# A two-layer hybrid decoder on one core: bonus and bias folded into the value projection, shorter roots, A blocks ahead of the output, r's loads first

## The chip, the cores and the metric

One core of a Trainium2 chip runs the whole kernel. The metric is the device time of one execution in microseconds (us), the median of several runs; a separate execution is recorded by the profiler. The engines are TensorE (PE, with its weight loads as PEld), VectorE (DVE), ScalarE (ACT), GpSimd (POOL) and SyncE (SP), whose queue starts most of the DMA transfers; ACT and POOL have DMA queues of their own.

## The reference

1024 tokens of width 1024 pass two layers, everything in float32. Layer 0 is RWKV-7 time mixing and a squared-ReLU MLP, layer 1 is causal attention with forget gates on shared keys and values and a second MLP. What the change touches:

```python
rkv = jnp.einsum('pbtd,pde->pbte', jnp.stack([x_r, x_k, x_v]), w_rkv)
...
y = (y - mean) * lax.rsqrt(var + GN_EPS)
y = y.reshape(B, T, D) * lnx_w.astype(f32) + lnx_b.astype(f32)
bonus = jnp.sum(r_h * k_h * r_k.astype(f32), axis=-1, keepdims=True) * v_h
y = (y + bonus.reshape(B, T, D)).astype(h.dtype) * g
return y @ w_o
```

Here `y` is the output of the recurrence over tokens (16 heads with a 64x64 state each), normalized per head; the bonus is one number per token and head times v. Keys and queries of the attention layer are normalized per head too, `rmsnorm(k, k_norm_g)`.

## The kernel before

Every float32 product is done as three matmuls of numbers split in two parts: a rounded part (`hi`, `whi`; made by ACT, L744) and the rest (`lo`, `wlo`; a subtraction, L747, on an engine that the caller names). The stages follow one another, and each engine works through its own queue in order. A scheduler makes these queues from the program's order and priorities, and for parts of the kernel (`k.pe`, the recurrence among them) PE keeps the order in which the program is written.

- **Start (0 to 84 us).** x's eight row blocks are loaded, each is normalized (`rsqrt_small`, L86 to L92: v = x*scale + eps, ACT's Ln and Exp, and four DVE steps that refine the root), transposed by PE (L889), and projected.
- **k and r (84 to 325).** Projections in blocks of 128 columns (`proj_pairs`, matmuls at L838). For each block of k, POOL, DVE and ACT make decays (`E`), scaled keys (`KK`, `kr`, `BK`) and the small matrices `N`, which go to DRAM (`d_E`, `d_KR`, `d_BK`, `d_N`). For each block of r, `prep_receptance` loads `Er` and `kr` (L286, L289; tiles of which three exist), `receptance` multiplies r with Er (L299) and forms the bonus (L300; sums over a head by PE at L203, copied by ACT at L211, four copies a block). DVE also inverts triangular blocks there (L316, L318: `Nb`, `Tb`, `Tm`, loaded at L309). SP's queue holds the loads and stores of all of this. In r and v the subtraction `wlo` is made by POOL; in k by DVE.
- **v (325 to 421).** `proj_tokens` (L858) computes 256 columns (g) for 256 tokens (b) at a time; `emit_v` copies them out (L975) and stores them in `d_v`. Beside it, DVE and ACT make the mixed input of the gates (`xg`; `t` at L923 and L924, `hi`, `lo`).
- **Recurrence (459 to about 745).** 16 chunks of 64 tokens. PE's order in a chunk c is: `pp`, `yp` from `KRz` (`rec_solve`; the state's part of the output), a transpose `tp`, `sa`, blocks `ap` of the next chunk (`rec_blocks`; DVE masks them into `AE`, L429), `u` (`rec_state`; DVE adds St into Z, L503; POOL scales St, L508), `yp` from `AE` (`rec_out`, the rest of the output), the second half of the blocks `ap`, and then `op` (`rec_corner`), which needs `AE`. Then DVE and POOL normalize the output (`rec_norm`: sum `m` L531, scaling L532, subtraction L533, root L86 to L92, product L540; on POOL the weight L541, the bias lnb L542, v times bonus L543, the sum L544), and POOL scales `KRz` for the next chunk (L455), as DVE scales AE (L455). From the fourth chunk on PE has 24 matmuls of the output projection (`wo`) per chunk to fill with, before that some of the gates (`gp`). `psA`, `psC` and `psY` are PSUM pools.
- **Keys, queries, values (1440 to 1644).** Products in Strassen form. `leave` copies a finished half (ACT), `emit` normalizes it per head (`hss`, `hrs`, L1708 to L1712: two feature halves, each with a root of its own) and has it transposed (L370) after four more products. Weights are scaled by the norm's gain in `w`, on engines that the string "wg" lists, otherwise DVE (L77).
- **Attention (1660 to 1895).** Head pairs: `b` and `d` hold the gate's bias (`dg` made by POOL, L1946), scores `s`, maximum `mx` (DVE, L1836), softmax on ACT, transposes `pt`.

The table that names engines for this stage has one letter per operation: v, s and p for DVE, ACT and POOL. The functions touched:

Of the kernel before, what the change touches and what calls it, by code (L numbers as in the profile page):

```python
# [56 lines left out]
        "wl": "vpvpvpvvvvpvpv", "wf": "pvvvvpvv", "wg": "vvvpvvsvvvvvssss"},  # L57
# [22 lines left out]
def rsqrt_small(k, pool, out, x, scale, eps, tag=""):  # L80

    nc = k.nc
    shape = list(x.shape)
    v = pool.tile(shape, F32, tag="rs_v" + tag, name="rs_v")
    t = pool.tile(shape, F32, tag="rs_t" + tag, name="rs_t")
    nc.vector.tensor_scalar(v, x, scale, eps, op0=ALU.mult, op1=ALU.add)  # L86
    nc.scalar.activation(t, v, AF.Ln)
    nc.scalar.activation(out, t, AF.Exp, scale=-0.5)
    nc.vector.tensor_tensor(t, v, out, op=ALU.mult)
    nc.vector.tensor_tensor(t, t, out, op=ALU.mult)  # L90
    nc.vector.tensor_scalar(t, t, -0.5, 1.5, op0=ALU.mult, op1=ALU.add)
    nc.vector.tensor_tensor(out, out, t, op=ALU.mult)  # L92


def make_consts(k):
    nc = k.nc
    cp = k.const
    k.ident = cp.tile([P, P], F32, name="ident")
    make_identity(nc, k.ident)

# [53 lines left out]
def rwkv_keep(k):  # L154

    cp, dr = k.const, k.dram

    k.sc = cp.tile([P, NK, NCH], F32, name="sc")
    k.ns2 = cp.tile([P, NK, NCH], F32, name="ns2")
    k.bon = cp.tile([P, NK, NCH], F32, name="bon")  # L160
    k.d_KR = dr.tile([NCH, P, NK, 2, C], F32, name="d_KR")
    k.d_BK = dr.tile([NCH, P, NK, 2, C], F32, name="d_BK")

    k.d_N = [dr.tile([2, P, 32, 32], F32, name=f"d_N{i}") for i in range(2)]
    k.d_E = [dr.tile([P, HC, C + 1], F32, name=f"d_E{i}") for i in range(2 * NK)]
    k.d_T = dr.tile([NK * 64, 32, 32], F32, name="d_T")
    k.d_B = dr.tile([NK * 64, 32, 32], F32, name="d_B")
# [90 lines left out]
def prep_pair(k, p, units):  # L258
# [10 lines left out]
    for h in range(2):  # L269
# [3 lines left out]
        for c in range(2):  # L273
            for d in range(2):
                s0 = u % 4 * 32 + (c * 2 + d) * HC
                q = 64 * c + 32 * d
                nc.sync.dma_start(k.d_N[p // 4][u // 4, s0:s0 + HC].rearrange("c i t -> i c t"),
# [4 lines left out]
def prep_receptance(k, p, hf, pool):  # L282

    cc = slice(HC * hf, HC * hf + HC)
    E = pool.tile([P, HC, C + 1], F32, tag="o", name="Er", bufs=3)
    k.nc.sync.dma_start(E, k.d_E[2 * p + hf])  # L286
    kt = pool.tile([P, HC, C], F32, tag="v", name="kr", bufs=3)
# [38 lines left out]
def rec_pools(k, ctx, a):  # L326
# [26 lines left out]
    k.lnb = k.rc.tile([P, NK, C], F32, name="lnb")  # L353
    for t, ap in ((k.lnw, a["rwkv_lnx_w"][0]), (k.lnb, a["rwkv_lnx_b"][0])):
# [165 lines left out]
def rec_norm(k, s):  # L520
# [5 lines left out]
    for h in range(2):  # L526
        nc.sync.dma_start(V[64 * h:64 * h + 64], k.d_v[cs, :].rearrange("t (p h v) -> h t p v", h=2, v=C)[h])
# [4 lines left out]
    nc.vector.tensor_scalar_mul(m, m, 1.0 / C)  # L532
    nc.vector.tensor_tensor(Y, yp, m.unsqueeze(2).broadcast_to(S3), op=ALU.subtract)  # L533
# [8 lines left out]
    nc.gpsimd.tensor_tensor(Y, Y, k.lnb, op=ALU.add)  # L542
    nc.gpsimd.tensor_tensor(V, V, k.bon[:, :, c:c + 1].broadcast_to(S3), op=ALU.mult)  # L543
# [21 lines left out]
def stage_recurrence(k, a, tile_of, gates):  # L565
    nc, tc = k.nc, k.tc
    with ExitStack() as ctx:
# [107 lines left out]
        for c in range(NCH):  # L675
# [18 lines left out]
            rec_out(k, cur, Z)  # L694
            if more:
                prepare(nxt, "b")
                hook()
            with tc.issue_after(k.gate_end.ins) if c == 0 else nullcontext():
                rec_norm(k, cur)
# [197 lines left out]
def stage_mix(k, a, right):  # L897
# [5 lines left out]
    with ExitStack() as ctx, ExitStack() as prep:  # L903
# [53 lines left out]
        loads = [prep_receptance(k, 0, hf, tp_) for hf in range(2)]  # L957

        def emit_r(e, o):
            with tc.high_priority(offset=PRIO):  # L960
# [5 lines left out]
                beside(nc.scalar.copy, k.bon[:, e], head_sums(k, kr))  # L966
            if e == 1:
                prep_inverse(k, 0)
        proj_pairs(k, ps, xr, wr[0], emit_r, nc.gpsimd)
        prep_inverse(k, 1)  # L970
        xv = mix(3)

        def emit_v(g, b, o):
            tv = tp_.tile([P, 2, 256], F32, tag="v", name="tv", bufs=3)
            nc.scalar.copy(tv, o)  # L975
            nc.scalar.dma_start(k.d_v[256 * b:256 * b + 256, 256 * g:256 * g + 256].rearrange("(j t) e -> t j e", t=P), tv)
# [6 lines left out]
        proj_tokens(k, bank, xv, wr[2], emit_v, nc.gpsimd)  # L983
# [618 lines left out]
def proj_seven(k, ps, p0, p1, p2, pool, w_tile, tick, X, w, gain, emit, number):  # L1602
# [3 lines left out]
    for h in range(2):  # L1606
        t = w_tile()
        nc.sync.dma_start(t, w[512 * h:512 * h + 512].rearrange("(k p) e -> p k e", p=P))
        for i in range(NK // 2):
            g = gain[:, 4 * h + i:4 * h + i + 1]  # L1610
            scale_on(k, ENG["q"]["wg"][8 * number + 4 * h + i] if number < 2 else "v", t[:, i], t[:, i], g)
# [67 lines left out]
def stage_qkv(k, a, xt, xs, raw, p0, W, late):  # L1679
    nc, tc, ps = k.nc, k.tc, k.ps  # L1680
    with ExitStack() as ctx:
# [17 lines left out]
        def heads_T(dst, gcol, f0):  # L1699

            def emit(fh, th, Cb):
                with tc.high_priority(offset=PRIO):
                    ss = sp.tile([P, 2, 8], F32, tag="hss", name="hss")
                    o3 = [Cb[:, b].rearrange("p (h n) -> p h n", n=N) for b in range(2)]
                    for b in range(2):
                        sq = pool.tile([P, 8, N], F32, tag="hsq", name="hsq", bufs=1)
                        nc.scalar.activation(sq, o3[b], AF.Square)
                        nc.vector.tensor_reduce(ss[:, b], sq, axis=AX.X, op=ALU.add)  # L1708
                    rs = sp.tile([P, 2, 8], F32, tag="hrs", name="hrs")
                    rsqrt_small(k, sp, rs, ss, 1.0 / N, 1e-6)  # L1710
                    for b in range(2):
                        nc.vector.tensor_tensor(o3[b], o3[b], rs[:, b].unsqueeze(2).broadcast_to([P, 8, N]), op=ALU.mult)  # L1712
# [11 lines left out]
                later.append([4, turn])  # L1724
# [46 lines left out]
        def leave(th, o):  # L1771
            C = [pool.tile([P, 2, 512], F32, tag="C", name="C", bufs=3) for _ in range(2)]
            for t in range(4):
                for fh in range(2):
                    nc.scalar.copy(C[fh][:, t // 2, 256 * (t % 2):256 * (t % 2) + 256], o[t][:, 256 * fh:256 * fh + 256])
            for fh in range(2):
                emit(fh, th, C[fh])
# [22 lines left out]
def stage_attention(k, a, op):  # L1800
# [4 lines left out]
    with ExitStack() as ctx:  # L1805
        lp, pp, vp, dp, bp, kp, kk = (ctx.enter_context(tc.tile_pool(name="t_" + n, bufs=b, reuse_waits="tile"))
                                      for n, b in (("l", 4), ("p", 2), ("v", 2), ("d", 3), ("b", 3), ("k", 2), ("kk", 2)))
# [316 lines left out]
```

## Time and profile before

| | us |
|---|---|
| median of 3 runs | 2620.12 (2620.12 to 2621.7) |
| profiled execution | 2622.44 |
| its span | 2620.7 |
| PE busy / idle in the span | 2531.1 / 89.6 |
| DVE busy | 1854.4 |
| ACT busy | 1236.3 |
| POOL busy | 508.1 |

The profile lists times from the start of the span, each engine's groups of instructions by line (`out<-in` by the program's names), and in the view of waits, for each engine, what it waited for and how long. Idle time of an engine that is not the bottleneck costs nothing by itself. `PEclk` is the granted share of PE's full clock; its mean here is 0.987. L numbers are lines of the kernel before unless the text speaks of the changed one; all of them moved by a few lines with the change (L367 became L374, L429 L436, L455 L462, L747 L751).

### The profile page before, as it was taken

The page shows a single profiled execution, that of the slowest core. Times are in us where ns is not written, and L with a number is a line of the kernel's source. Part 1 is how long each engine was busy: PE and PEld are TensorE (multiplying, and loading weights), DVE is VectorE, ACT ScalarE, POOL GpSimd, SP SyncE. Part 2 cuts the span into 40 slices and gives each one's busy share as a digit, 9 for nine tenths or more (in the row PEclk, how much of TensorE's full clock was granted, in tenths as well). Part 3 has the DMA queues.
Part 4 walks back from the last instruction along what each step waited for, and adds up shares of the span by engine and source line. Part 5 has one row for each costly group of instructions (what it writes and reads, how often), then busy time and mean ns, then how long its engine had stood idle before and what let it go on. Part 6 is the DMA issues. An engine that isn't in the chain of part 4 may idle for free.

```text
span 2620.7 us, 44642 instructions
## 1 busy us (share of the span) xinstructions
PE 2531.1 (97%) x17601; PEld 2135.2 (81%) x17601; DVE 1854.4 (71%) x2959; ACT 1236.3 (47%) x2126; POOL 508.1 (19%) x393
## 2 busy tenths in 40 slices
PE   7999999799999999999999899999999999999999
PEld 4887798677888888888888899887887888878887
DVE  6667874888877777566678777687726877746675
ACT  4763325423355455443455434587725555544332
POOL 2012123766710000001201122343300000000120
PEclk9999999899999999999999999999999999999999
DMA  4466754865426453766642312755242654476663
GB/s 130 112 163 170 202 153 123 222 162 161 122 54 202 140 174 120 281 224 229 237 146 68 110 67 83 199 144 151 76 149 56 202 170 140 138 262 224 227 210 140
DMA packets 412261, 415.41 MB, mean 159 GB/s; under 512 B 189770, under 2 KB 297506, under 8 KB 412052
## 3 DMA queue, kind: packets, MB, share of 16 engines
q1 hardware_dynamic: 399092, 387.26, 48.1%
q10 hardware_dynamic: 8832, 12.65, 1.4%
q0 software_dynamic: 4128, 12.66, 1.3%
q8 instruction: 138, 2.26, 0.4%
q14 instruction: 71, 0.58, 0.1%
HBM read 292.76 MB, written 119.73 MB: 157 GB/s over the span
## 4 chain that ended last, share of the span: by engine, by line
PE 77%; DVE 7%; issue 5%; DMA 4%; POOL 3%; ACT 2%; SPq 1%; POOLq 0%; DVEq 0%; ACTq 0%
PE mm L367 37%; PE mm L780 7%; PE mm L781 7%; PE mm L782 7%; PE mm L838 4%; PE mm L858 4%; PE tp L370 3%; PE s L367 2%; PE o L367 2%; PE wo L367 1%; PE z1p L1025 1%; PE sums L203 1%; POOL KRz L455 1%; DMA Vh<-d_v 1%; DMA b<-d_c 1%
## 5 line engine op out<-in xcount | busy, mean ns | idle before, releaser
L367 PE MATMUL mm<-oh 128*128 128x512 f32 x896 | 349.2, 390 | 1.3 <-ACT oh L744 1.3
L367 PE MATMUL mm<-ol,oh 128*128 128x512 f32 x896 | 349.1, 390 | 1.4 <-DVE ol L747 1.4
L367 PE MATMUL mm<-oh,ol 128*128 128x512 f32 x896 | 349.5, 390 | 0.8 <-DVE ol L747 0.6
L744 ACT CAST oh<-ra 128x1024 fp32r<-128x1024 f32 x108 | 113.8, 1054 | 336.0 <-PE mm L367 238.5
L747 DVE TENSOR_TENSOR ol<-ra,oh 128x1024 fp32r<-128x1024 f32 x108 | 137.9, 1277 | 126.1 <-ACT oh L744 126.1
L367 PEld LDWEIGHTS mm<-oh 128*128 128x128 f32 x896 | 168.6, 188 | 36.8 <-ACT oh L744 1.7
L367 PEld LDWEIGHTS mm<-oh,ol 128*128 128x128 f32 x896 | 168.6, 188 | 36.5 <-DVE ol L747 1.5
L367 PEld LDWEIGHTS mm<-ol,oh 128*128 128x128 f32 x896 | 168.5, 188 | 36.6 <-DVE ol L747 1.7
L780 PE MATMUL mm<-xhT,ah 128*128 128x512 f32 x448 | 174.3, 389 | 0.0
L781 PE MATMUL mm<-xlT,ah 128*128 128x512 f32 x448 | 174.3, 389 | 0.0
L782 PE MATMUL mm<-xhT,al 128*128 128x512 f32 x448 | 174.3, 389 | 0.0
L1527 POOL DMA_DIRECT2D xt<-d_xh x8 | 4.4, 552 | 754.9 <-DMA rb<-in_mlp_w_out_dram 421.2
L744 ACT CAST ah<-w 128x512 fp32r<-128x512 f32 x128 | 79.2, 620 | 109.5 <-PE mm L781 98.3
L780 PE MATMUL mm<-xhB,ah 128*128 128x512 f32 x336 | 130.7, 389 | 0.0
L781 PE MATMUL mm<-xlB,ah 128*128 128x512 f32 x336 | 130.7, 389 | 0.0
L782 PE MATMUL mm<-xhB,al 128*128 128x512 f32 x336 | 130.7, 389 | 0.0
L747 DVE TENSOR_TENSOR ol<-rb,oh 128x1024 fp32r<-128x1024 f32 x92 | 120.9, 1314 | 1.4 <-ACT oh L744 1.4
L1843 ACT ACTIVATE l<-l,mx 128x512 f32<-128x512 f32 (+7 forms) x128 | 99.2, 776 | 36.5 <-DVE mx L1840 36.1
L1300 ACT ACTIVATE z<-z 128x512 f32<-128x512 f32 x112 | 70.8, 633 | 74.2 <-DVE z L1297 72.8
L838 PE MATMUL mm<-hi,whi 128*128 128x512 f32 x256 | 89.0, 412 | 10.0 <-DVE Er L299 7.9
L782 PEld LDWEIGHTS mm<-xhT,al 128*128 128x128 f32 x448 | 84.1, 188 | 17.6
L780 PEld LDWEIGHTS mm<-xhT,ah 128*128 128x128 f32 x448 | 84.1, 188 | 17.4
(488 smaller groups left out, 6952.8 us busy)
## 6 DMA issues: line engine op xcount, KB each, us to landing
rb<-in_mlp_w_out_dram SPq DMA_DIRECT2D x124, 512.0 KB, 5.5
ra<-d_H SPq DMA_DIRECT2D x108, 512.0 KB, 4.0
w<-in_mlp_w_in_dram SPq DMA_DIRECT2D x64, 512.0 KB, 4.2
d_H<-z SPq DMA_DIRECT2D x56, 512.0 KB, 3.7
d_H<-sums SPq DMA_DIRECT2D x32, 768.0 KB, 5.6
raw<-in_rwkv_w_rkv_dram SPq DMA_DIRECT2D x24, 512.0 KB, 4.1
KRz<-d_KR SPq DMA_DIRECT2D x16, 512.0 KB, 5.0
KRz<-d_BK SPq DMA_DIRECT2D x16, 512.0 KB, 5.3
```

The lines of the kernel that those rows point to most:

```text
L203: k.nc.tensor.matmul(sums[:, c], flat(xs[c // 4][:, 2 * (c % 4):2 * (c % 4) + 2]), k.heads, start=True, stop=True)
L367: return self.tc.keep_in_program_order(self.tc.nc.tensor.matmul(*args, **kw))
L370: return self.tc.keep_in_program_order(self.tc.nc.tensor.transpose(*args))
L744: nc.scalar.copy(hi, src)
L747: lo_eng.tensor_tensor(lo, src, hi.bitcast(F32), op=ALU.subtract)
L780: te.matmul(out, ah, bh, start=i == 0, stop=False)
L781: te.matmul(out, ah, bl, start=False, stop=False)
L782: te.matmul(out, al, bh, start=False, stop=i == n - 1)
L838: nc.tensor.matmul(o[e][half], wt[:, i % 4, es], xs[i][part][:, 512 * half:512 * half + 512], start=i == 0 and wt is hi and part == 0, sto ...
L858: k.nc.tensor.matmul(o[:, j], x[:, ts], y, start=j == 0 and i == 0 and n == 0, stop=j == 1 and i == NK - 1 and n == 2)
L1300: nc.scalar.activation(x, x if o is None else o, AF.Relu)
L1843: nc.scalar.activation(l, l, AF.Exp, bias=m, scale=-1.0, accum_out=SM[:, j, qb:qb + 1])
```

## The change

- The root has one DVE step less, and its first DVE step no longer stands ahead of Ln: ACT adds eps itself.
- The bonus stays as `bon` with one copy per block, v times bonus plus lnb is made in `emit_v` for each piece of v and stored in `d_vb`, and the recurrence loads `d_vb` in place of `d_v`. POOL's L542 and L543 go.
- The mean's scaling (L532) is joined with the subtraction.
- `prepare(nxt, "b")` (the second half of the blocks) stands ahead of `rec_out`.
- r's first loads have tiles of their own and a high priority; the stores of N for p >= 6 go to ACT's queue; `wlo` in r and v is made by DVE.
- In the keys/queries stage the scalings of w are ACT's, the two feature halves of the second row half share one norm and a tile of their own, and their transposes wait for five and six products in place of four.
- The attention's pool `d` has four places in place of three.

```diff
         "spvv", "T3l": "vpvp", "T4h": "ssss", "T4l": "vpvp", "B22h": "vsss", "B22l": "vvpp", "wh": "spspsssssssvss",
-        "wl": "vpvpvpvvvvpvpv", "wf": "pvvvvpvv", "wg": "vvvpvvsvvvvvssss"},
+        "wl": "vpvpvpvvvvpvpv", "wf": "pvvvvpvv", "wg": "ssssssssssssssss"},
 }
...
     t = pool.tile(shape, F32, tag="rs_t" + tag, name="rs_t")
-    nc.vector.tensor_scalar(v, x, scale, eps, op0=ALU.mult, op1=ALU.add)
-    nc.scalar.activation(t, v, AF.Ln)
+    nc.scalar.activation(t, x, AF.Ln, scale=scale, bias=k.eps[eps][0:shape[0]])
+    nc.vector.tensor_scalar(v, x, -0.5 * scale, -0.5 * eps, op0=ALU.mult, op1=ALU.add)
     nc.scalar.activation(out, t, AF.Exp, scale=-0.5)
-    nc.vector.tensor_tensor(t, v, out, op=ALU.mult)
-    nc.vector.tensor_tensor(t, t, out, op=ALU.mult)
-    nc.vector.tensor_scalar(t, t, -0.5, 1.5, op0=ALU.mult, op1=ALU.add)
-    nc.vector.tensor_tensor(out, out, t, op=ALU.mult)
+    nc.vector.tensor_tensor(v, v, out, op=ALU.mult)
+    nc.vector.tensor_tensor(v, v, out, op=ALU.mult)
+    nc.vector.scalar_tensor_tensor(out, v, 1.5, out, op0=ALU.add, op1=ALU.mult)
...
     make_identity(nc, k.ident)
+    k.eps = {e: cp.tile([P, 1], F32, name=f"eps{i}") for i, e in enumerate((1e-6, 64e-5))}
+    for e, t in k.eps.items():
+        nc.vector.memset(t, e)
...
     k.ns2 = cp.tile([P, NK, NCH], F32, name="ns2")
-    k.bon = cp.tile([P, NK, NCH], F32, name="bon")
+    k.bon = cp.tile([P, NK, H], F32, name="bon")
+    k.d_vb = dr.tile([T, D], F32, name="d_vb")
     k.d_KR = dr.tile([NCH, P, NK, 2, C], F32, name="d_KR")
...
                 q = 64 * c + 32 * d
-                nc.sync.dma_start(k.d_N[p // 4][u // 4, s0:s0 + HC].rearrange("c i t -> i c t"),
+                (nc.scalar if p >= 6 else nc.sync).dma_start(k.d_N[p // 4][u // 4, s0:s0 + HC].rearrange("c i t -> i c t"),
                                   N_[q:q + 32, :, 32 * d:32 * d + 32])
...
     cc = slice(HC * hf, HC * hf + HC)
-    E = pool.tile([P, HC, C + 1], F32, tag="o", name="Er", bufs=3)
+    if p < 0:
+        pool, o, v, n = k.pi, "Er", "kr", 2
+    else:
+        o, v, n = "o", "v", 3
+    E = pool.tile([P, HC, C + 1], F32, tag=o, name="Er", bufs=n)
     k.nc.sync.dma_start(E, k.d_E[2 * p + hf])
-    kt = pool.tile([P, HC, C], F32, tag="v", name="kr", bufs=3)
+    kt = pool.tile([P, HC, C], F32, tag=v, name="kr", bufs=n)
     for h, hs in enumerate(HALF):
...
     k.lnw = k.rc.tile([P, NK, C], F32, name="lnw")
-    k.lnb = k.rc.tile([P, NK, C], F32, name="lnb")
-    for t, ap in ((k.lnw, a["rwkv_lnx_w"][0]), (k.lnb, a["rwkv_lnx_b"][0])):
+    for t, ap in ((k.lnw, a["rwkv_lnx_w"][0]),):
         v = ap.rearrange("(p h v) -> h p v", h=2, v=C)
...
     for h in range(2):
-        nc.sync.dma_start(V[64 * h:64 * h + 64], k.d_v[cs, :].rearrange("t (p h v) -> h t p v", h=2, v=C)[h])
+        nc.sync.dma_start(V[64 * h:64 * h + 64], k.d_vb[cs, :].rearrange("t (p h v) -> h t p v", h=2, v=C)[h])
     yp = s["yp"]
...
     nc.vector.tensor_reduce(m, yp, axis=AX.X, op=ALU.add)
-    nc.vector.tensor_scalar_mul(m, m, 1.0 / C)
-    nc.vector.tensor_tensor(Y, yp, m.unsqueeze(2).broadcast_to(S3), op=ALU.subtract)
+    nc.vector.scalar_tensor_tensor(Y, m.unsqueeze(2).broadcast_to(S3), -1.0 / C, yp, op0=ALU.mult, op1=ALU.add)
     sq = w1.tile(S3, F32, tag="ysq", name="ysq")
...
     nc.gpsimd.tensor_tensor(Y, Y, k.lnw, op=ALU.mult)
-    nc.gpsimd.tensor_tensor(Y, Y, k.lnb, op=ALU.add)
-    nc.gpsimd.tensor_tensor(V, V, k.bon[:, :, c:c + 1].broadcast_to(S3), op=ALU.mult)
     nc.gpsimd.tensor_tensor(Y, Y, V, op=ALU.add)
...
             squares()
-            rec_out(k, cur, Z)
             if more:
...
                 hook()
+            rec_out(k, cur, Z)
             with tc.issue_after(k.gate_end.ins) if c == 0 else nullcontext():
...
         head_mask(k, k.pi)
-        loads = [prep_receptance(k, 0, hf, tp_) for hf in range(2)]
+        with tc.high_priority(offset=GP):
+            loads = [prep_receptance(k, 0, hf, tp_) for hf in range(2)]
...
                         loads.append(prep_receptance(k, e + 1, hf, tp_))
-                beside(nc.scalar.copy, k.bon[:, e], head_sums(k, kr))
+                nc.scalar.copy(k.bon[:, :, 2 * e:2 * e + 2], head_sums(k, kr))
             if e == 1:
                 prep_inverse(k, 0)
-        proj_pairs(k, ps, xr, wr[0], emit_r, nc.gpsimd)
+        proj_pairs(k, ps, xr, wr[0], emit_r, nc.vector)
         prep_inverse(k, 1)
         xv = mix(3)
+        lnb = k.pi.tile([P, D], F32, name="lnb")
+        nc.sync.dma_start(lnb, a["rwkv_lnx_b"].broadcast_to([P, D]))
...
             nc.scalar.copy(tv, o)
+            vb = k.pi.tile([P, 2, 4, N], F32, tag="vb", name="vb", bufs=2)
+            if g < 2:
+                for j in range(2):
+                    for h in range(4):
+                        nc.scalar.mul(vb[:, j, h], tv[:, j, N * h:N * h + N], k.bon[:, 2 * b + j, 4 * g + h:4 * g + h + 1])
+            else:
+                nc.vector.tensor_tensor(vb, tv.rearrange("p j (h v) -> p j h v", v=N),
+                                        k.bon[:, 2 * b:2 * b + 2, 4 * g:4 * g + 4].unsqueeze(3).broadcast_to([P, 2, 4, N]),
+                                        op=ALU.mult)
+            vb = vb.rearrange("p j h v -> p j (h v)")
+            nc.vector.tensor_tensor(vb, vb, lnb[:, 256 * g:256 * g + 256].unsqueeze(1).broadcast_to([P, 2, 256]), op=ALU.add)
+            nc.sync.dma_start(k.d_vb[256 * b:256 * b + 256, 256 * g:256 * g + 256].rearrange("(j t) e -> t j e", t=P), vb)
             nc.scalar.dma_start(k.d_v[256 * b:256 * b + 256, 256 * g:256 * g + 256].rearrange("(j t) e -> t j e", t=P), tv)
...
             return pool.tile([P, 512], F32, tag=tag, name="mm")
-        proj_tokens(k, bank, xv, wr[2], emit_v, nc.gpsimd)
+        proj_tokens(k, bank, xv, wr[2], emit_v, nc.vector)
         prep.close()
...
             g = gain[:, 4 * h + i:4 * h + i + 1]
-            scale_on(k, ENG["q"]["wg"][8 * number + 4 * h + i] if number < 2 else "v", t[:, i], t[:, i], g)
+            scale_on(k, ENG["q"]["wg"][8 * number + 4 * h + i] if number < 2 else "s", t[:, i], t[:, i], g)
         A[f"A1{h + 1}"], A[f"A2{h + 1}"] = t[:, :, 0:256], t[:, :, 256:512]
...
-            def emit(fh, th, Cb):
+            def norm(Cs):
                 with tc.high_priority(offset=PRIO):
-                    ss = sp.tile([P, 2, 8], F32, tag="hss", name="hss")
-                    o3 = [Cb[:, b].rearrange("p (h n) -> p h n", n=N) for b in range(2)]
-                    for b in range(2):
+                    n = len(Cs)
+                    o3 = [C[:, b].rearrange("p (h n) -> p h n", n=N) for C in Cs for b in range(2)]
+                    ss = sp.tile([P, 2 * n, 8], F32, tag=f"hss{n}", name="hss")
+                    for o, s in zip(o3, range(2 * n)):
                         sq = pool.tile([P, 8, N], F32, tag="hsq", name="hsq", bufs=1)
-                        nc.scalar.activation(sq, o3[b], AF.Square)
-                        nc.vector.tensor_reduce(ss[:, b], sq, axis=AX.X, op=ALU.add)
-                    rs = sp.tile([P, 2, 8], F32, tag="hrs", name="hrs")
-                    rsqrt_small(k, sp, rs, ss, 1.0 / N, 1e-6)
-                    for b in range(2):
-                        nc.vector.tensor_tensor(o3[b], o3[b], rs[:, b].unsqueeze(2).broadcast_to([P, 8, N]), op=ALU.mult)
+                        nc.scalar.activation(sq, o, AF.Square)
+                        nc.vector.tensor_reduce(ss[:, s], sq, axis=AX.X, op=ALU.add)
+                    rs = sp.tile([P, 2 * n, 8], F32, tag=f"hrs{n}", name="hrs")
+                    rsqrt_small(k, sp, rs, ss, 1.0 / N, 1e-6, tag=f"{n}")
+                    for o, s in zip(o3, range(2 * n)):
+                        nc.vector.tensor_tensor(o, o, rs[:, s].unsqueeze(2).broadcast_to([P, 8, N]), op=ALU.mult)
+            def emit(fh, th, Cb, wait=4, normed=False):
+                if not normed:
+                    norm([Cb])
...
                         nc.sync.dma_start(dst[f:f + P, 512 * th:512 * th + 512], t)
-                later.append([4, turn])
+                later.append([wait, turn])
+            emit.norm = norm
             return emit
...
         def leave(th, o):
-            C = [pool.tile([P, 2, 512], F32, tag="C", name="C", bufs=3) for _ in range(2)]
+            if th:
+                C2 = k.rz.tile([P, 2, 2, 512], F32, tag="KRz0", name="C")
+            C = [C2[:, fh] if th else pool.tile([P, 2, 512], F32, tag="C", name="C", bufs=3) for fh in range(2)]
             for t in range(4):
...
                     nc.scalar.copy(C[fh][:, t // 2, 256 * (t % 2):256 * (t % 2) + 256], o[t][:, 256 * fh:256 * fh + 256])
+            emit.norm(C)
             for fh in range(2):
-                emit(fh, th, C[fh])
+                emit(fh, th, C[fh], 5 + th, True)
         o = [mm("mm") for _ in range(4)]
...
         lp, pp, vp, dp, bp, kp, kk = (ctx.enter_context(tc.tile_pool(name="t_" + n, bufs=b, reuse_waits="tile"))
-                                      for n, b in (("l", 4), ("p", 2), ("v", 2), ("d", 3), ("b", 3), ("k", 2), ("kk", 2)))
+                                      for n, b in (("l", 4), ("p", 2), ("v", 2), ("d", 4), ("b", 3), ("k", 2), ("kk", 2)))
         sp = ctx.enter_context(tc.tile_pool(name="t_s", bufs=6, reuse_waits="tile"))
```

## The prediction

> **What bounds the kernel now.** I read the page first: busy times, then the chain that ended last.
>
> ```profile
> PE 2531.1 (97%) x17601; PEld 2135.2 (81%) x17601; DVE 1854.4 (71%) x2959; ACT 1236.3 (47%) x2126; POOL 508.1 (19%) x393
> PE 77%; DVE 7%; issue 5%; DMA 4%; POOL 3%; ACT 2%; SPq 1%; POOLq 0%; DVEq 0%; ACTq 0%
> ```
>
> TensorE is the bound, with 89.6 us of idle time in a span of 2620.7. The change takes no matmul of weight away, so all it can win is idle time and the slow matmuls that follow it. The second view is therefore PE's waits, asked stage by stage: the start (0 to 84), the k and r projections (84 to 325), the recurrence (470 to 800), the keys/queries projections (1356 to 1470), and the first attention scores (1655 to 1672).
>
> ```profile
> PE tp L889 <- DVE x L879: 7.4, 5, 3.0
> ...
> PE mm L838 <- DVE Er L299: 7.9, 2, 4.6
> PE sums L203 <- DVE kr L300: 1.6, 1, 1.6
> ...
> PE yp L367 <- POOL KRz L455: 10.6, 12, 1.3
> PE op L367 <- DVE AE L429: 8.4, 7, 3.4
> PE u L367 <- DVE Z L489: 1.2, 2, 0.8
> PE yp L367 <- DVE Z L489: 1.2, 2, 0.8
> ...
> PE tp L370 <- DVE C L1712: 7.9, 1, 7.9
> ...
> PE s L367 <- DVE mx L1836: 2.8, 1, 2.8
> ```
>
> The columns are total us, times, longest. Together the waits in reach are 7.4 + 9.5 + 21.4 + 7.9 + 2.8 = 49.0 us. The third view, busy time by stretch, shows the price behind a wait in the column PEclk (after PE, PEld, DVE, ACT and POOL):
>
> ```profile
> 230.00:325.00 95.00, 85.54 (x432) 70.60 (x422) 78.27 (x112) 21.78 (x43) 17.16 (x9) 0.91 0.79 205
> 325.00:421.00 96.00, 95.77 (x800) 95.56 (x799) 67.06 (x82) 35.16 (x49) 25.48 (x13) 1.00 0.48 144
> 470.00:620.00 150.00, 133.10 (x2418) 109.04 (x2414) 130.37 (x197) 48.42 (x120) 105.46 (x87) 0.95 0.68 182
> 568.00:573.00 5.00, 5.00 (x82) 4.48 (x80) 0.90 (x2) 0.58 (x1) 3.21 (x4) 0.66 0.40 123
> 1459.00:1464.00 5.00, 4.28 (x23) 3.97 (x24) 2.82 (x7) 1.37 (x2) 0.00 (x0) 0.58 0.25 94
> 1660.00:1670.00 10.00, 7.07 (x32) 5.81 (x31) 5.09 (x20) 3.44 (x10) 3.12 (x3) 0.73 1.05 323
> ```
>
> From 568 to 573 PE is busy throughout, yet at a clock of 0.66: 5 x 0.34 = 1.7 us lost, right behind two waits for KRz. The same sum gives at most 95 x 0.09 = 8.6 us in r, 150 x 0.05 = 7.5 in the recurrence, 5 x 0.42 = 2.1 at the keys and 10 x 0.27 = 2.7 at the first scores, 20.9 in all; part of it lies inside the idle time itself. So waits and clock hold at most about 70 us.
>
> **Start.** Each of eight row blocks runs a root between its load and its transposes; of its five DVE steps, one moves beside ACT's Ln and one goes.
>
> ```profile
> L86 DVE TENSOR_SCALAR rs_v<-ss 128x1 f32<-128x1 f32 x8 | 1.2, 146 | 7.5 <-ACT junk L876 7.5
> ```
>
> Two such steps are 0.3 us a block, times the five waits 1.5; bounds 0 (x's loads set the pace) and 3 (both steps in every block and no other wait late). I take 1.5.
>
> **r's projection.** SP's queue, around r's first loads; Er and kr are what r is multiplied with, d_N and Nb belong to the inverses. Before:
>
> ```order
> 85 L309 DMA Nb<-d_N_89 128x2x1024
> 86 L277 DMA d_N_90<-KK 32x8x32 x8
> 87 L301 DMA d_KR<-Er 128x8x64 x2
> 88 L763 DMA raw<-in_rwkv_w_rkv_dram 128x4x256
> 89 L254 DMA d_BK<-BK 64x8x64
> 90 L252 DMA d_BK<-BK 64x8x128
> 91 L254 DMA d_BK<-BK 64x8x64
> 92 L286 DMA Er<-d_E_93 128x520
> ```
>
> and now:
>
> ```order
> 85 L309 DMA d_KR<-Er 128x8x64 x2
> 86 L248 DMA d_KR<-KK 128x8x64
> 87 L294 DMA Er<-d_E_98 128x520
> 88 L297 DMA kr<-d_BK 64x8x64 x2
> 89 L256 DMA d_BK<-BK 64x8x128
> 90 L258 DMA d_BK<-BK 64x8x64 x2
> ```
>
> The eight stores of d_N (and eight more behind) go to ACT's queue and Er passes Nb, so the loads whose lateness showed as idle DVE come earlier. The price of POOL's splits (wlo) is seen on DVE: the same form with and without one beside it.
>
> ```profile
> L316 DVE TENSOR_TENSOR Tm<-Nb,Tb 128x62 f32<-128x62 f32 (+15 forms) x36 | 22.2, 616 | 1.3 <-DMA Nb<-d_N 0.6
> L318 DVE TENSOR_TENSOR Tb<-Tb,Tm 128x62 f32<-128x62 f32 (+15 forms) x35 | 17.7, 505 | 0.9
> L747 DVE TENSOR_TENSOR lo<-t,hi 128x1024 fp32r<-128x1024 f32 x6 | 7.3, 1221 | 4.0 <-ACT hi L744 4.0
> L299 DVE TENSOR_TENSOR Er<-mm,Er 128x512 f32<-128x512 f32 x10 | 6.6, 684 | 1.8 <-DMA Er<-d_E 1.8
> ...
> 261.29 2.42 POOL L747 TENSOR_TENSOR wlo<-raw,whi 128x1024 fp32r<-128x1024 f32 x1 [0.33 <-ACT whi L744]
> ...
> 254.99 0.75 DVE L300 SCALAR_TENSOR_TENSOR kr<-Er,cols,kr 128x512 f32<-128x512 f32 x1
> 258.65 2.86 DVE L300 SCALAR_TENSOR_TENSOR kr<-Er,cols,kr 128x512 f32<-128x512 f32 x1 [1.60 <-DMA kr<-d_BK]
> 261.44 2.82 DVE L316 TENSOR_TENSOR Tm<-Nb,Tb 128x510 f32<-128x510 f32 x1
> ```
>
> PE's longest wait (4.6, for Er) lies behind these two stretched steps and a late kr: 2.1 of stretch in the first (2.86 against 0.75), as much in the second, + 1.6 of DMA, against 2 x 1.22 for two splits now on DVE itself, so 3.4 of 4.6 go. The other wait for Er (7.9 - 4.6 = 3.3) was for a load and goes; of the 1.6 for kr I take half. That is 7.5 of 9.5, and half of the 8.6 of clock: 11.8. Bounds: 0 and 18.1.
>
> **v's projection.** DVE gets what POOL had and more. Twelve splits from 230 on at 1.22 are 14.6; vb takes 8 products and 16 sums of 128x512 at 0.684, 16.4; the stretch returns at least 22.2 - 17.7 = 4.5. 78.27 + 67.06 + 31.0 - 4.5 = 171.8 on DVE in 191 us less the 12 saved, 179: no longer idle, but still below PE. PE has no idle time to speak of here (95.77 of 96), so there is only loss to take: splits queue in order behind vb, and a late one stops PE. I take 2, bounds 0 and 8 (two waits like the mean 3.95 for Er). The 64 scalings that ACT does for the first two column blocks have cover: ACT is busy 35.16 of 96. The lnb load, the 16 stores of vb on SP and the bonus copies (one in place of four) I cost at nothing: no PE wait here is for them, DMA works at 0.48; without that cover chunk 0's normalization would come late by one load.
>
> **Recurrence.** PE in one of the early chunks (ap: the next chunk's A block; yp: this chunk's output; op: the first matmul on that block). Before:
>
> ```order
> 1842 L370 MATMUL tp<-ident,KRz_4226 128x128 x4
> 1843 L367 MATMUL u<-Z,BKt 64x64 x16
> 1844 L367 MATMUL yp<-Z,AE 64x64 x16
> 1845 L367 MATMUL ap<-KRz_4226 128x128 x8
> 1846 L367 MATMUL op<-B_4671,AE 32x32 x16
> ```
>
> and now:
>
> ```order
> 1823 L377 MATMUL tp<-ident,KRz_4321 128x128 x4
> 1824 L374 MATMUL u<-Z,BKt 64x64 x16
> 1825 L374 MATMUL ap<-KRz_4321 128x128 x8
> 1826 L374 MATMUL yp<-Z,AE 64x64 x16
> 1827 L374 MATMUL op<-B_4759,AE 32x32 x16
> ```
>
> Between ap and op now stands yp, and on DVE AE comes ahead of the normalization's first steps:
>
> ```order
> 487 L436 TENSOR_TENSOR AE<-ap,mask 128x4x128 x2
> 488 L510 TENSOR_TENSOR Z<-u,St 64x8x64 x2
> 489 L436 TENSOR_TENSOR AE<-ap,mask 128x4x128 x2
> 490 L538 TENSOR_REDUCE m<-yp 128x8
> 491 L462 TENSOR_TENSOR AE<-KRz_4321,sc 64x8x64 x2
> ```
>
> ```profile
> L531 DVE TENSOR_REDUCE m<-yp 128x8 f32<-128x512 f32 x16 | 11.1, 692 | 1.7 <-PE yp L367 1.2
> L532 DVE TENSOR_SCALAR m<-m 128x8 f32<-128x8 f32 x16 | 5.9, 371 | 0.5
> L543 POOL TENSOR_TENSOR Vh<-Vh,bon 128x512 f32<-128x512 f32 x16 | 17.8, 1112 | 56.4 <-DMA Vh<-d_v 56.3
> L542 POOL TENSOR_TENSOR Y<-Y,lnb 128x512 f32<-128x512 f32 x16 | 21.2, 1324 | 1.3
> ...
> 567.84 1.14 PE L367 MATMUL yp<-Z,KRz 64*64 64x64 f32 x30 [1.14 <-POOL KRz L455]
> ```
>
> Before, m, its scaling and a subtraction of m's size stood between Z and that second AE, 0.69 + 0.37 + 0.69 = 1.8 us. Now AE is ready about 1.3 us (two at 0.684) behind Z, and yp covers about 1.1 of it (as long as the yp in the last row); I take 6.4 of op's 8.4, and leave 2.0.
>
> POOL scales KRz behind V times bonus, which itself waited 56.3 us for its loads over 16 chunks, 3.5 each; that product and the sum with lnb (2.4 a chunk together) are gone. A wait of 1.1 with 3.5 + 2.4 us of slack won should vanish: 10.6, of which I take 9.0, and 0.6 of the 2.4 for Z, since nothing on sa's side changes. Clock: a bit over a quarter of 7.5, 2.0, because single waits stay. Sum 18; bounds 8 (only POOL's waits, less something new) and 28.9.
>
> **Keys and queries.** The 7.9 is for the norm of a product's second half; DVE does two scalings of w and two roots on the way. The scalings go to ACT (busy 12 us of 30 there), the root becomes one, and the transposes stand one or three products later. All 7.9 can go, plus 2.1 of clock; but the next product's split on DVE is then next, so I take 8; bounds 3 and 10.
>
> **Attention's first scores.** The pool of d grows by one, and b's first loads move ahead of raw's on SP.
>
> ```profile
> POOL dg L1946 <- DMA b<-d_c: 13.4, 3, 9.8
> ...
> DVE l L1836 <- POOL dg L1946: 2.9, 2, 2.5
> ```
>
> The 2.8 of PE was DVE waiting for dg, which waited for b. No row shows what DVE's later places do; I take 3, between -1 and 5.5.
>
> **Sum.** 1.5 + 11.8 - 2 + 18 + 8 + 3 = 40.3. The profiled execution took 2622.44, its span 2620.7 with 1.7 around it; 2622.4 - 40.3 = 2582.1; the median of the runs is 2.3 lower, so 2580 for a median.
>
> A rule weighed: the Trainium skill, "TensorE: Matmul & The Clock Gate", section on the HAM clock gate, lets the clock fall after at least one idle window of about 3.4 us. The trace shows it at 0.66 behind two waits of 1.1 us or less. By the page only the waits of 4.6 and 7.9 would cost clock; r's 4.3 of clock would fall to a third of 8.6, 2.9, and the 2.0 in the recurrence and about 1.0 at the first scores to nothing, and the time would be 4 higher, 2584.
>
> **Rivals.** (1) The r gain is eaten: DVE, at 172 of 179, passes PE's waits on from Er to the splits, and r and v give -2 in place of 9.8: 2592. For it speaks that share; against it, that DVE also stood idle for loads that now come earlier. With a second stage at its lower bound (recurrence 8): 2602. (2) All of the waits and clock go: 70 less the 7.4 - 1.5 that hangs on x's loads, 64: 2556. (3) Slower: each weight piece whose split comes late on DVE stops PE like a wait for Er did, 3.95 plus a third of 8.6, 6.8 us. The other terms give 30.5, and r nothing; from five of the sixteen pieces on it is slower. At seven, 47.6 - 30.5 = 17 over: 2637. Against it: pieces are split ahead of use, and v's stage had DVE idle for 29 us. (4) The moves could fail to be what they say; the rows above show them made.
>
> **Chances.** Forecast 0.58 (own range 2570 to 2590), rival 1 0.25 (2590 to 2606), rival 2 0.09, rival 3 0.04, no difference 0.04 (rival 1 with recurrence and keys at nothing). A measurement of this kernel tells 0.2%, 5 us, from nothing. The range runs from 2562, which leaves half of rival 2 out, to 2604. Faster 0.92, same 0.04, slower 0.04.
>
> **What would show it.** Right: no wait of op for AE over 1 us, none of yp for KRz, none of tp for C, PEclk near 1.00 from 470 to 620, DVE without stretched L300 in r. Wrong: PE in v's stage waiting for wlo, or Z's waits grown by what op and KRz lost.

## The result and the profile after

The changed kernel takes 2580.82 us (median of 4 runs, 2578.5 to 2581.26) against 2620.74 (now 4 runs too, 2620.12 to 2621.7): a ratio of 0.9846, 95% interval 0.9829 to 0.9863. The profiled execution took 2581.26, its span 2579.1. The head of its page:

```profile
span 2579.1 us, 44650 instructions
PE 2518.7 (98%) x17601; PEld 2127.1 (82%) x17601; DVE 1796.6 (70%) x2893; ACT 1268.7 (49%) x2198; POOL 407.4 (16%) x345
```

PE executes the same 17601 matmuls. It idles 60.4 us in place of 89.6, 29.2 less, and it is busy 12.4 us less with the same work. That is the clock: its record in the trace holds only full and half speed, and half speed for 70.7 us before and 40.6 now (a part of both while PE idles). PE's waits after, for the same five stretches as in the prediction (start; k and r; recurrence; keys and queries; first scores):

```profile
PE tp L893 <- DVE x L883: 7.2, 5, 2.8
...
PE sums L207 <- DVE kr L308: 2.8, 1, 2.8
PE mm L842 <- DVE Er L307: 1.0, 1, 1.0
...
PE sa L374 <- ACT Ps L484: 5.0, 3, 2.9
PE pp L374 <- DVE AE L462: 3.2, 4, 1.1
PE op L374 <- DVE AE L436: 1.6, 4, 0.5
PE yp L374 <- POOL KRz L462: 0.7, 1, 0.7
...
PE tp L377 <- DVE xhT L70: 0.5, 1, 0.5
...
PE s L374 <- DVE mx L1867: 0.8, 1, 0.8
```

The waits for Er, KRz, AE (by op) and C are gone or small; the one for kr in r grew from 1.6 to 2.8. Two waits that were small or absent stand in the recurrence now: sa for Ps, and pp for the scaled AE. Before, the first of them was, in the whole stage:

```profile
PE sa L367 <- ACT Ps L477: 3.3, 2, 2.2
```

Busy time and clock after, in r (the first row starts 7.6 us ahead of it), v, the first 150 us of the recurrence, and the first scores:

```profile
217.70:313.00 95.30, 91.07 (x545) 76.11 (x544) 76.01 (x127) 23.09 (x31) 2.93 (x7) 0.95 0.79 201
313.00:409.00 96.00, 96.00 (x803) 95.96 (x802) 82.50 (x117) 50.58 (x108) 11.28 (x9) 1.00 0.55 176
457.50:607.50 150.00, 142.06 (x2672) 117.27 (x2669) 117.97 (x194) 54.45 (x129) 85.10 (x79) 0.99 0.80 194
1618.00:1628.00 10.00, 8.32 (x56) 7.06 (x54) 5.46 (x21) 2.87 (x9) 1.09 (x1) 1.00 1.03 294
```

The clock is 0.99 in the recurrence (0.95 before) and DVE, in v, is busy 82.50 of 96: fuller, and PE loses nothing to it.

For the experiments I cut both traces at PE's own instructions, from the start of one named matmul to the start of another in the timeline:

| stretch of PE | before | after | change |
|---|---|---|---|
| start, to the first `z1p` | 34.0 | 32.6 | -1.5 |
| k, to the last `L` | 195.3 | 192.7 | -2.6 |
| r, to v's first matmul | 95.8 | 87.9 | -7.9 |
| v and gates, to the first `ap` | 118.4 | 117.9 | -0.5 |
| recurrence, to the last `wo` | 310.6 | 294.5 | -16.1 |
| first MLP, to the last `tp` of UV | 601.5 | 601.5 | 0.0 |
| keys and queries, to the last `tp` of C | 288.0 | 277.1 | -10.9 |
| values, to the first `s` | 17.4 | 18.4 | +1.0 |
| first scores, to the first `o` | 12.6 | 9.1 | -3.5 |
| rest of the attention | 219.7 | 221.9 | +2.2 |
| all behind it | 722.2 | 720.3 | -1.9 |

How much of this is chance shows in the kernels below, where no edit touches a stretch. The first MLP agrees within 0.1 us, keys and queries within 0.1 in kernels with the change there and within 1.3 in kernels without it. But r ran from 87.3 to 90.0 with the change (93.2 to 95.8 without), the recurrence from 293.2 to 295.8, once 299.1 (308.6 and 310.6 without), the rest of the attention from 218.3 to 223.2, and the time behind it also varied by about 4. A stage is therefore compared by its own stretch, a difference inside these ranges is not read, and neither is a total of a few us. Each stretch comes from the one profiled execution of its kernel.

### The profile page after: what moved, and what is told of

It is laid out like the page before. It is cut to its first block, busy times and chain, and to the rows that moved or that the text cites. A ratio compares the mean times of both kernels' runs of the same rounds, so it can differ in the third digit from the quotient of the medians.

```text
span 2579.1 us, 44650 instructions
## 1 busy us (share of the span) xinstructions
PE 2518.7 (98%) x17601; PEld 2127.1 (82%) x17601; DVE 1796.6 (70%) x2893; ACT 1268.7 (49%) x2198; POOL 407.4 (16%) x345
## 4 chain that ended last, share of the span: by engine, by line
PE 85%; DVE 5%; DMA 4%; issue 3%; ACT 2%; POOL 1%; SPq 1%; POOLq 0%; ACTq 0%; DVEq 0%
PE mm L374 38%; PE mm L785 7%; PE mm L786 7%; PE mm L784 7%; PE mm L842 5%; PE mm L862 4%; PE wo L374 3%; PE tp L377 3%; PE s L374 1%; PE o L374 1%; PE yp L374 1%; PE sums L207 1%; PE z1p L1046 1%; DMA b<-d_c 1%; PE ap L374 1%
## 5 line engine op out<-in xcount | busy, mean ns | idle before, releaser
L785 PEld LDWEIGHTS mm<-xlT,ah 128*128 128x128 f32 x448 | 84.1, 188 | 17.5
```

Of the source, the lines that this page charges most:

```text
L785: te.matmul(out, ah, bl, start=False, stop=False)
```

## The experiments

Theory: three places lost time to queues in order, each on its own (Er and kr in r; KRz and AE in the recurrence; C at the keys), and the edits add up as in the sum. Rivals stand with each run.

**r: the splits.** Changed kernel, one edit:

```diff
-        proj_pairs(k, ps, xr, wr[0], emit_r, nc.vector)
+        proj_pairs(k, ps, xr, wr[0], emit_r, nc.gpsimd)
-        proj_tokens(k, bank, xv, wr[2], emit_v, nc.vector)
+        proj_tokens(k, bank, xv, wr[2], emit_v, nc.gpsimd)
```

> The changed kernel with the splits wlo of r and v back on POOL. Theory (a split on POOL stretches what DVE does beside it, and a wait of PE for Er or kr follows): 3 to 5 us slower than the changed kernel, about 2584 to 2586, with steps of DVE of 2.8 us where 0.7 is usual in r, and PE's waits in r at 6 us or more in place of 4.2. Rival (DVE was nearly full in r and v, so taking 20 us of splits off it helps more than the stretch costs): 1 to 4 us faster, 2577 to 2580.

Measured: 2591.35 (2588.34 to 2593.21), slower than the changed kernel by 10.5. PE's waits in r and v, then two of DVE's steps beside a POOL split (kr, with the next kr for comparison, and Tb, with a Tm of the same shape), then the clock in the stretch that follows:

```profile
PE sums L207 <- DVE kr L308: 7.2, 2, 5.2
...
318.88 2.37 POOL L751 TENSOR_TENSOR wlo<-raw,whi 128x1024 fp32r<-128x1024 f32 x1 [3.72 <-ACT whi L748]
...
319.02 2.77 DVE L308 SCALAR_TENSOR_TENSOR kr<-Er,cols,kr 128x512 f32<-128x512 f32 x1
323.58 0.74 DVE L308 SCALAR_TENSOR_TENSOR kr<-Er,cols,kr 128x512 f32<-128x512 f32 x1
...
336.21 2.68 POOL L751 TENSOR_TENSOR wlo<-raw,whi 128x1024 fp32r<-128x1024 f32 x1 [14.97 <-ACT whi L748]
...
336.11 0.52 DVE L324 TENSOR_TENSOR Tm<-Nb,Tb 128x350 f32<-128x350 f32 x1
336.66 2.61 DVE L326 TENSOR_TENSOR Tb<-Tb,Tm 128x350 f32<-128x350 f32 x1
...
326.00:350.00 24.00, 24.00 (x186) 24.00 (x187) 22.45 (x34) 8.81 (x19) 2.76 (x2) 0.91 0.30 85
```

The stretch is there (2.77 where the same step takes 0.74, 2.61 where the same shape takes 0.52), and the rival falls. But the price is twice the expected and lies elsewhere: r is 88.6 against 87.9, k is 194.4 against 192.7, and v is 124.2 against 117.9. The wait of 2.1 for the stretched kr of the lines above falls into v's beginning, with 6.8 us of half speed behind it.

The same edit in the other direction, alone, in the kernel before (nc.gpsimd to nc.vector at both places):

> The kernel before with one edit: the splits wlo of r and v on DVE. Theory (splits on POOL stretch DVE's steps, and PE's waits for Er and kr follow): r's stage 4 to 6 us shorter, v's stage the same, 2614 to 2617. Rival (the waits were for loads, whatever the splits do): r's stage within 1.5 us of before, 2619 to 2622.

Measured: 2610.77 (2609.69 to 2611.35), ratio 0.996 (0.9947 to 0.9972). r is 87.6, 8.2 us shorter than before and as short as in the changed kernel; k, whose end meets r's first split, is 192.9 against 195.3. One wait for Er stays:

```profile
PE mm L838 <- DVE Er L299: 3.8, 1, 3.8
```

So the splits alone give what r gained, more than the theory gave them. They explain k's gain too: a wait of 2.1 for kt in k stands in the kernel before and in the run with the splits on POOL, and neither in this run nor in the changed kernel. And they make DVE less busy, not more. From r's start to the first `ap`, first the kernel before, then this run (DVE's time is the third behind the length of the stretch):

```profile
229.30:443.50 214.20, 204.51 (x1349) 181.01 (x1347) 153.95 (x201) 65.80 (x104) 48.74 (x30) 0.96 0.61 166
226.40:431.90 205.50, 200.88 (x1347) 178.84 (x1345) 146.79 (x217) 65.86 (x104) 16.70 (x19) 0.98 0.65 174
```

DVE takes 16 steps more and is busy 7.2 us less (over the whole span 1844.9 against 1854.4).

**r: the loads.** Changed kernel, the loads and stores as before:

```diff
-        with tc.high_priority(offset=GP):
-            loads = [prep_receptance(k, 0, hf, tp_) for hf in range(2)]
+        loads = [prep_receptance(k, 0, hf, tp_) for hf in range(2)]
...
-                (nc.scalar if p >= 6 else nc.sync).dma_start(k.d_N[...
+                nc.sync.dma_start(k.d_N[...
```

> The changed kernel with r's first loads at the usual priority and in the shared tiles, and all stores of N on SP's queue again. Theory (the lateness of Er and kr in SP's queue was half of r's waits): 4 to 8 us slower than the changed kernel, 2585 to 2589, all of it between 218 and 313. Rival (the loads were hidden behind DVE's queue, and r's gain comes from the splits alone): within 1 us of 2581.

Measured: 2581.48 (2578.15 to 2585.48). r is 89.5, 1.7 longer, with a wait for Er of 2.8 and 4.1 in all; k is 2.0 shorter. The total is the rival's. The recurrence came out 4.7 longer here, 2.4 of it one idle time of PE that nothing in the profile released; I leave it unexplained. The theory's half for the loads falls: r's 89.5 lies among the 87.3 to 90.0 of kernels with the early loads, and k and r together take 280.2 against 280.6. Where the splits are on DVE, no gain of the early loads can be told.

**Recurrence: the order.** Changed kernel, `rec_out` ahead of `prepare(nxt, "b")` again:

```diff
+            rec_out(k, cur, Z)
             if more:
                 prepare(nxt, "b")
                 hook()
-            rec_out(k, cur, Z)
```

> The changed kernel with the output's matmuls ahead of the second half of the A blocks again, the rest as changed. Theory (in the early chunks op waits for AE, 8.4 us before and 1.6 now): 4 to 8 us slower, 2585 to 2589, with PE's waits of op for AE at 5 us or more and PEclk under 0.97 between 460 and 510. Rival (POOL's relief alone gave the recurrence's gain): within 1 us of 2581.

Measured: 2583.24 (2578.72 to 2584.95). The recurrence is 301.6 against 294.5, 7.2 longer. The total shows 2.4, less than the 4 to 8 expected, since the rest of the attention ran 3.5 shorter and the stretches ahead of v 2.6. PE's waits there, and 50 us of its early chunks:

```profile
PE sa L374 <- ACT Ps L484: 7.4, 4, 2.9
PE op L374 <- DVE AE L436: 6.4, 8, 1.3
...
455.00:505.00 50.00, 39.80 (x813) 33.48 (x809) 40.66 (x60) 21.73 (x47) 35.74 (x27) 0.93 0.84 209
```

op's wait is back at 6.4 and the clock at 0.93 (0.97 in the changed kernel from 457 to 507). Theory, in its stage.

**Recurrence: POOL.** Changed kernel with the bias and v times bonus back in `rec_norm`, and v's stage without vb:

```diff
+    nc.gpsimd.tensor_tensor(Y, Y, k.lnb, op=ALU.add)
+    nc.gpsimd.tensor_tensor(V, V, k.bon[:, :, c:c + 1].broadcast_to(S3), op=ALU.mult)
     nc.gpsimd.tensor_tensor(Y, Y, V, op=ALU.add)
```

> The changed kernel with v times bonus and the bias back on POOL in the recurrence, and the v stage without vb; the order of the blocks as changed. Theory (KRz came late because POOL stood behind V's loads): PE's waits of yp for KRz come back at 8 to 10 us, the recurrence is 8 to 10 us longer, v's stage is the same within 1 us, in all 2588 to 2591. Rival (the order of blocks alone made the difference, since yp comes later than before): 2580 to 2582.

Measured: 2600.07 (2598.29 to 2604.54). The wait is as expected:

```profile
PE yp L374 <- POOL KRz L462: 9.7, 12, 1.3
```

but the recurrence is 310.2, 15.7 longer than in the changed kernel and as long as before. PE's idle time there, 22.9 against 14.7, explains 8.2 of it and the clock, 0.97 over the stage against 0.99, most of the rest (315 x 0.02 = 6.3). v with its gates takes 117.9 with and without vb. r came out 93.0, 5.1 longer, with a wait of 6.5 for kr; the edit also brings back four copies of bon per block and takes lnb's load out, and which of them does it, or whether it is chance, was not tried. That the order then gives nothing at all was not expected, so the order alone was tried in the kernel before (the edit of the run with the output first, reversed):

> The kernel before with one edit: the second half of the A blocks ahead of the output's matmuls. Theory of additive gains (op's waits for AE go, as the prediction had it): the recurrence 6 to 8 us shorter, 5 to 8 us under the kernel before. Rival (with POOL late by its bonus product, the time saved ahead of op is waited out at KRz): the recurrence within 2 us of before, PE's waits of yp for KRz up from 10.6 by several us, no change that can be told.

Measured: 2613.96 (2607.95 to 2623.93), ratio 0.9972 (0.9961 to 0.9983). The profiled execution, at 2607.95, is the fastest of eleven. The recurrence is 300.0 there, 10.6 shorter, and the wait for KRz fell, which neither theory had:

```profile
PE yp L367 <- POOL KRz L455: 2.4, 4, 0.8
```

POOL's queue shows a difference that fits. First the run before (bonus back, order changed), then this one:

```profile
603.88 1.06 POOL L549 TENSOR_TENSOR Vh<-Vh,bon 128x512 f32<-128x512 f32 x1 [3.82 <-DMA Vh<-d_v]
604.89 3.00 POOL L515 TENSOR_TENSOR St<-Z,sc 64x512 f32<-64x512 f32 x2
607.97 2.21 POOL L462 TENSOR_TENSOR KRz<-KRz,sc 64x512 f32<-64x512 f32 x2
```

```profile
598.10 1.05 POOL L508 TENSOR_TENSOR St<-Z,sc 64x512 f32<-64x512 f32 x1
602.08 1.06 POOL L543 TENSOR_TENSOR Vh<-Vh,bon 128x512 f32<-128x512 f32 x1 [2.92 <-DMA Vh<-d_v]
603.21 1.39 POOL L508 TENSOR_TENSOR St<-Z,sc 64x512 f32<-64x512 f32 x1
604.68 2.52 POOL L455 TENSOR_TENSOR KRz<-KRz,sc 64x512 f32<-64x512 f32 x2
```

The scheduler, given the new order, put one half of St ahead of the product that waits for V. Both halves behind it cost 6.3 us from the product's start to KRz's end, one half 5.1. So this run changes two things, and what the order is worth by itself it cannot say. What POOL is worth without the order, the run that takes only the product away can say (kernel before; v is added without the bonus, which is left out of the result):

```diff
-    nc.gpsimd.tensor_tensor(V, V, k.bon[:, :, c:c + 1].broadcast_to(S3), op=ALU.mult)
```

> The kernel before without the product of v and bonus on POOL; it adds v itself, so the bonus is left out of the result. The order of the blocks is as before. Theory (POOL stood behind V's loads ahead of St and KRz): PE's waits of yp for KRz fall from 10.6 to under 2 us and the recurrence is 8 to 11 us shorter, 2609 to 2613. Rival (op's wait for AE takes over what KRz's gives): the recurrence 0 to 3 us shorter.

Measured: 2615.39 (2609.43 to 2617.5), ratio 0.9976 (0.9966 to 0.9986). No wait for KRz is left in the list, the recurrence is 301.7, 8.9 shorter, and op's wait rose from 8.4 to 10.6, with a low clock around it:

```profile
PE op L367 <- DVE AE L429: 10.6, 17, 2.2
...
465.00:515.00 50.00, 41.62 (x799) 34.80 (x796) 40.91 (x63) 22.50 (x47) 33.52 (x27) 0.83 0.86 223
```

In its stage, the theory's 8 to 11; the total stays above the expected 2609 to 2613. POOL's relief without the order gives 8.9 here and 8.9 in the run with the output first; the order on top of it gives 7.2. With both, 16.1. The shorter root and the joined mean were not undone by themselves, but the run with the output first has both and takes 301.6, and this one has neither and takes 301.7.

**Keys and queries.** Three edits, undone one at a time in the changed kernel. (In the kernel both row halves have the shared norm and the later transposes, five products for the first and six for the second; only the tile of its own is the second's alone.) The scalings:

```diff
-... "wg": "ssssssssssssssss"},
+... "wg": "vvvpvvsvvvvvssss"},
...
-            scale_on(k, ... if number < 2 else "s", t[:, i], t[:, i], g)
+            scale_on(k, ... if number < 2 else "v", t[:, i], t[:, i], g)
```

> The changed kernel with the scalings of the weights in the keys/queries stage on their old engines (DVE, most of them). Theory (DVE's relief by scalings and roots is what took the 7.9 us wait away): PE waits for DVE there again, 3 to 6 us, 2584 to 2587. Rival (the later place of the transposes alone did it): no wait over 1 us between 1348 and 1460, 2580 to 2582.

Measured: 2581.48 (2578.39 to 2583.74); the stage takes 278.7, 1.6 longer, a wait of tp for xhT of 1.9 against 0.5. Neither fits: not the 3 to 6, and not nothing. The transposes' place:

```diff
-                emit(fh, th, C[fh], 5 + th, True)
+                emit(fh, th, C[fh], 4, True)
```

> The changed kernel with the second row half's transposes after four products again, the shared norm and ACT's scalings kept. Theory (DVE's relief took the wait away): a wait of tp for C of 1 us or less, 2580 to 2582. Rival (the place did it): tp waits 4 to 8 us for C and the clock falls once behind it, 2586 to 2591.

Measured: 2579.38 (2577.82 to 2580.23); the stage takes 277.1, as changed, so the rival falls. The place gives nothing in this stage and costs 1.0 in the next: the values take 17.4 here, as before the change, and in the two other runs with four products, and 18.4 in every run with five and six. The norm, each half apart (`emit(fh, th, C[fh])`, C from its old pool):

```diff
-            emit.norm(C)
             for fh in range(2):
-                emit(fh, th, C[fh], 5 + th, True)
+                emit(fh, th, C[fh])
```

> The changed kernel with the two feature halves of the keys/queries stage normalized apart, each with its own root and old tiles, and transposed after four products; ACT's scalings and the shorter root kept. Theory (any one of the three edits there is enough, since DVE needs to come some 8 us earlier at one place only): no wait of tp for C over 1.5 us, 2580 to 2582. Rival (the shared norm is what did it): tp waits 4 to 8 us, 2585 to 2591.

Measured: 2589.68 (2582.7 to 2590.69); the stage takes 286.3, 9.2 longer:

```profile
PE tp L377 <- DVE C L1734: 5.5, 1, 5.5
...
1420.00:1460.00 40.00, 34.54 (x270) 34.09 (x269) 32.00 (x55) 18.81 (x35) 9.08 (x4) 0.91 0.11 40
```

The rival: 9.2 of the 10.9 come back with the norms apart. This edit undoes the shared root, the order of the norm's steps, the tile of its own and the place together, and of these only the place was tried by itself; which of the others carries it is open. One of the four executions took 2582.7, so the wait may not come in each.

**First scores.** `("d", 4)` back to `("d", 3)`:

> The changed kernel with three places for d in the attention. Theory (the places make b's first loads free earlier): the first scores wait 2 to 3 us for DVE and the clock is about 0.7 there, 3 to 5 us slower up to the first output of the attention, 2583 to 2586. Rival (b's loads moved for other reasons): the stage starts as in the changed kernel, 2580 to 2582.

Measured: 2580.54 (2579.6 to 2583.91). The first scores take 11.7 against 9.1, and PE waits as before the change:

```profile
PE s L374 <- DVE mx L1867: 2.8, 1, 2.8
```

The theory's wait, with less of the slow clock (0.89 from 1618 to 1628, where 0.7 was expected); the total does not show the 2.6 us, which is less than it varies by.

**A further step.** lnb loaded from ACT's queue behind r's fifth block, and the transposes after four products:

```diff
+            if e == 4:
+                with tc.issue_after(done.ins):
+                    nc.scalar.dma_start(lnb, a["rwkv_lnx_b"].broadcast_to([P, D]))
```

> The changed kernel with lnb loaded from ACT's queue behind the fifth block of r, and the transposes after four products. Theory (lnb's 512 KB stand between r's loads on SP while DMA works at 0.79, and the wait of 2.8 for kr and the slow clock behind it follow): r's stage 2 to 5 us shorter, 2575 to 2579. Rival (kr waits for the store of d_KR, which lnb does not hold up): r's stage within 1 us, 2579 to 2581.

Measured: 2578.06 (2575.15 to 2579.95). r takes 87.2 against 87.9, and kr's wait is 2.4 against 2.8: the rival. Of the lower total, 1.0 is the values' stretch (the transposes' place) and the rest lies in stretches that vary anyway; it is no version shown to be faster than the changed kernel.

## Why the prediction was right

The forecast was 2580 for a median of 2580.82. By its own steps:

- **Start**, 1.5 taken: 1.5 measured, but not where it was placed. PE's waits for x, which the term stood on, fell only from 7.4 to 7.2, and 1.0 of the gain is an earlier load ahead of the first matmul (8.4 to 7.4), which the root does not touch. From the first matmul on, the four kernels with the old root took 24.7 to 25.8 and the ten with the shorter one 23.5 to 25.2; no run undoes the root by itself.
- **r**, 11.8 taken: 7.9 measured in r, and 2.6 in k, for which the sum had no term. That PE waits behind DVE's stretched steps holds, the parts of the sum don't. I gave a good part of the waits to late loads; splits on DVE alone made r 8.2 and k 2.4 shorter, and of the early loads no gain can be told.
- **v**, a loss of 2 taken: a gain of 0.5, outside the bounds of 0 to 8. The term that was off is the stretch: I took 4.5 back for it against 14.6 of splits, and the run with the splits alone shows DVE busy 7.2 less with the splits than without them. In the changed kernel, with vb on top, DVE rose to 82.50 of 96 and stayed below PE, so rival 1 (r's gain eaten) fell.
- **Recurrence**, 18 taken: 16.1. KRz's waits fell from 10.6 to 0.7 (9.0 taken), op's from 8.4 to 1.6 (6.4 taken). What came instead, sa for Ps at 5.0 (3.3 in the whole stage before) and pp for AE at 3.2, was the "something new" of the lower bound. So PE's idle time in the stage fell by 11.5 (26.2 to 14.7), where the waits were taken at 16.0; half speed fell from 17.1 us to 6.8, up to 5.1 us of PE's time, where 2.0 was taken. The two errors cancel in part. Nor are the two edits a simple sum: each alone gives 9 to 10.6, and with POOL late the order gave nothing in one schedule and 10.6 in another that also moved St.
- **Keys and queries**, 8 taken: 10.9, above the upper bound of 10. PE's idle time in the stage fell from 9.1 to 0.5, with two small waits (0.8 and 0.2) that the bound left out, and its 6.8 us of half speed went. The next product's split, which I kept 2 us for, did not come late. Of the reasons I named, the scalings carry 1.6 and the place nothing; making the norm in one go, with its tile, carries the most.
- **First scores**, 3 taken: 2.5 measured with the stretch of values ahead of it (1.0 lost to the transposes' place, 3.5 won). The extra place of d gives 2.6.
- **Clock.** The sum held about 8.3 us of it (4.3, 2.0 and about 1 at each of two places); PE's busy time fell by 12.4. The other reading that was weighed, by which only the waits of 4.6 and 7.9 cost clock, would have given some 4 less than the sum; the recurrence before the change speaks against it: half speed began five times there, each time behind 3.41 us with 1.8 to 3.2 us of idle time. The Trainium skill, "TensorE: Matmul & The Clock Gate", section on the HAM clock gate, puts the fall to half speed behind at least one idle window of about 3.4 us. The traces agree on the half and on steps of 3.41 us, but such a step need not be idle throughout (last section).

That the total came within 1 us of the forecast is luck: 3.9 and 1.9 too much were taken in r and the recurrence, and 2.6, 2.5 and 2.9 too little in k, in v and at the keys.

## What to carry to other kernels

On a kernel bound by TensorE, list its waits by stage, the small ones too, and read the slow clock behind them from the clock's own record; together they tell about what edits of the other engines can win. Look in a queue for the instruction that waits for a DMA ahead of work that TensorE needs, and see with the scheduled order which of them passes it, since one moved line can reorder another engine too. Where several edits serve one wait, undo them one at a time: at the keys one of three carried most of it. Where work disturbs another engine, count what that engine loses to it before calling it too full to take the work over.

## What was not expected of the hardware

- Short waits lower the clock when several fall close together. In every trace here the clock is full or half, and it changes in steps of 3.41 us. From the kernel before, first a step in which PE idles 1.85 us in two waits (the longer 1.14) and the half-speed step behind it, then a step with 1.25 us of idle time and the full-speed step behind it (the share of the clock is the third number from the end):

```profile
565.45:568.86 3.41, 1.56 (x40) 1.27 (x36) 2.01 (x2) 0.58 (x1) 2.25 (x2) 1.00 0.63 142
568.86:572.27 3.41, 3.41 (x43) 2.92 (x42) 0.20 (x1) 0.58 (x1) 2.51 (x3) 0.50 0.53 164
...
585.93:589.34 3.41, 2.16 (x42) 1.79 (x44) 1.20 (x2) 0.07 (x1) 3.11 (x5) 1.00 0.49 161
589.34:592.75 3.41, 3.41 (x80) 3.05 (x80) 2.23 (x4) 1.24 (x3) 3.25 (x3) 1.00 0.88 305
```

  Counted over the recurrence in all fourteen traces, steps at full speed only: all 40 with 1.61 us or more of idle time were followed by half speed, none of the 1208 with 1.37 or less, and 4 of the 10 between. Elsewhere the border is less sharp: four steps after 110 us with 0.5 to 1.2 us of idle time were followed by half speed, and so was, in most traces, one near 94 us with none. So a wait has no fixed price in clock: before the change, the six waits for KRz after 620 us (5.2 us in all) cost none.
- A split of 128x1024 on POOL stretches one DVE step by about 2.1 us (0.52 to 2.61), more than the 1.22 us that DVE needs for the split itself. Moving the work onto the busier engine gained 10 us, and left that engine less busy.
